# Early blocks as plain float32 matmuls, and modulation products moved out of the second mixer

## The chip, the core and the metric

The kernel runs on one core of a Trainium2 chip. The metric is the device time of one execution in microseconds (us); lower is better. TensorE multiplies matrices, VectorE (DVE), ScalarE (ACT) and GpSimd (POOL) do the work around it, and SyncE (SP) issues the DMAs that bring the weights from memory.

## What is computed

A trunk of two layers for 256 tokens and a model width of 2048, all in float32. In each layer a vector `c` gives six modulation vectors, and two sublayers, a mixer and a feed-forward with a short convolution, are each fed with a normed and modulated x:

```python
for i in range(DEPTH):
    mod = (c_act @ ada_w[i] + ada_b[i])[:, None, :]
    sh1, sc1, g1, sh2, sc2, g2 = jnp.split(mod, 6, axis=-1)
    h = rms_norm(x, norm_g[i, 0]) * (1.0 + sc1) + sh1
    y = even_mixer(h, ...) if i % 2 == 0 else odd_mixer(h, ...)
    x = x + g1 * y
    h = rms_norm(x, norm_g[i, 1]) * (1.0 + sc2) + sh2
    x = x + g2 * conv_ffn(h, ...)
```

The first mixer is a convolution beside a sparse attention; the second is a sliding-window attention (projections q, k, v) beside a gated unit (projections u and v). The feed-forward is `(silu(a) * b) @ w_down`, where a and b are 44 blocks of 128 columns each of `h @ w_up`, passed through a convolution over three tokens.

## The kernel before

Activations stand transposed: x is 16 tiles of 128 channels by 256 tokens, `xT[:, kt]`. A product with a weight block of 128 columns takes 16 steps over kt and adds up in one PSUM bank of 128x256; there are eight banks.

**Split weights.** From the first feed-forward on, float32 accuracy comes from three matmuls of the type float32r: a weight piece `raw` of up to 1024 columns is copied to `whi` (ScalarE, line 133), the rest `raw - whi` goes to `wlo` (line 139, VectorE or, for a quarter of the columns, GpSimd), the activation is split likewise, and `mm_t` issues hi x hi, hi x lo and lo x hi (lines 346 to 348). A piece that is wanted with `split=False` is multiplied as it is, by one plain float32 matmul (line 350); the first mixer works so. `take()` hands out the next piece, splits two pieces ahead and loads further ahead; three buffers each hold `raw`, `whi` and `wlo`. A raw buffer of a split piece is free when the split is done, one of a plain piece when TensorE has read it.

**Early blocks.** A sublayer could begin only when all of x is known and normed. `Modulated.outer` (FIRST = 7 blocks) runs ahead of that: it multiplies x, scaled by its gain but not yet normed, with seven blocks of weights at once, kt on the outside, into seven banks; two further columns carry the shift. `raw(kt)` makes the scaled x in a tile `hr` (lines 475 to 478), one kt ahead. At kt 3 the tokens' sums of squares go through TensorE, at kt 5 the reciprocal roots are spread over the partitions (`on_all`, line 409, from the `diag` tiles of line 408), and from then on the normed `h` of the later blocks is made beside it in `begin` and `end` (`hn` line 520, `hf` line 523, `h` lines 526 and 531). Early blocks stand at the head of the first feed-forward, the second mixer (its u projection) and the second feed-forward.

**Modulation products.** Each of the 192 columns of the modulation is one DVE instruction over 128x2048 (line 269, `ada`), with a DMA of 1 MB into one of two buffers ahead of it. No planner places them: each `take()` adds `rate["ada"]`, a number per stage, to a credit, and a full credit emits one product. A product that is needed and not there is emitted on the spot (`modulation`). In `outer` the rate is zero.

The order on every engine is that of the program text; engines wait for each other by semaphores only. The feed-forward works in four quarters: `h` blocks (two passes over 16 kt per gated block), then 16 output tiles `g` from the quarter's gated blocks, each added into x with its gate (line 545).

Of the kernel before, what the change touches and what calls it, by code (L numbers as in the profile page):

```python
# [8 lines left out]
F32 = mybir.dt.float32  # L9
F32R = mybir.dt.float32r  # L10
I32 = mybir.dt.int32
AF = mybir.ActivationFunctionType
ALU = mybir.AluOpType
# [3 lines left out]
P = 128  # L17
D = 2048
T = 256
NT = 2  # L20
KD = D // P
# [2 lines left out]
NQ = 4  # L24
QK = KF // NQ
FIRST = 7
HEADS = 8
NC = 15
L = 32
# [21 lines left out]
STATS = 3  # L51
SPREAD = 2
ADA_O = 0.0
LO_O = 0.25
LO_A = 0.25
ADA_A = 0.25
CONV_A = 0
# [13 lines left out]
ADA_1 = 0.5  # L71
ADA_2 = 0.5
ADA_3 = 0.6
ADA_F0S = 0.4
ADA_F0U = 0.4
ADA_F0D = 0.2
ADA_L1 = 0.5
ADA_F1 = 0.2
CONV = 1.6
ADA_OUT = 0.45  # L80
LO_L1 = 0.25
# [71 lines left out]
def trunk(ctx, tc, a, out):  # L153
# [11 lines left out]
    def bank():  # L165
        return psum.tile([P, 512], F32, tag="bank", name="bank")
# [26 lines left out]

    def want_ffn(i):
        for k in range(KD // 2):
            W.want(a["wup1"][i, k], 2, FIRST * P)
        for b in range(2 * QK - FIRST):
            W.want(a["wup2"][i, b], KD, P)
        for q in range(NQ):
            for j in range(q * QK, (q + 1) * QK):  # L200
                if q:
                    for ab in range(2):
                        W.want(a["wup"][i, j - QK, ab], KD, P)
            for kt in range(KD):
                W.want(a["wdn"][i, q, kt], QK, P)
# [21 lines left out]
    want_out(0)  # L227
    want_ffn(0)
    for k in range(KD // 2):
        W.want(a["od_u1"][k], 2, FIRST * P)  # L230
    W.want(a["od_kv"], KD, 512)
    for c in range(2):
        W.want(a["od_q"][c], KD, 512)
    for c in range(2):
        W.want(a["od_v"][c], KD, 512)
    for c in range(8 - FIRST):
        W.want(a["od_u2"][c], KD, P)
    want_out(1)
    want_ffn(1)
# [207 lines left out]
    class Modulated:  # L447
# [18 lines left out]
        def raw(self, kt):  # L466

            while self.nraw <= min(kt + 1, KD - 1):
                n = self.nraw
                self.nraw += 1  # L470
                gs, sh = self.gain(n)
                x = xT[:, n]
                h = hm.tile([P, 4 * T], F32R, tag="hm", name="hr")[:, :2 * T + 4].rearrange("p (a b) -> p a b", a=2)
                h = h[:, :, :T + 2]
                S.activation(h[:, 0, :T], x, AF.Copy, scale=gs)
                S.activation(h[:, 0, T:], sh.to_broadcast([P, 2]), AF.Copy)  # L476
                V.scalar_tensor_tensor(h[:, 1, :T], x, gs, h[:, 0, :T].bitcast(F32), op0=ALU.mult, op1=ALU.subtract)
                V.tensor_sub(h[:, 1, T:], sh.to_broadcast([P, 2]), h[:, 0, T:].bitcast(F32))
                self.raws.append(h)
            return self.raws[kt]  # L480

        def outer(self, n):

            first = [bank()[:, :T + 2] for _ in range(n)]
            r = None
            ada_rate, rate["ada"] = rate["ada"], ADA_O
            share, W.share = W.share, LO_O
            for kt in range(KD):
                x = self.raw(kt)
                w, _ = take()  # L490
                if kt == STATS:
                    drain()
                    r = token_rstd()
                if kt == STATS + SPREAD:
                    self.bc = on_all(r)
                for b in range(n):
                    s_ = slice(b * P, (b + 1) * P)
                    mm_t(first[b], w, s_, x, kt == 0, kt == KD - 1)
                k0 = STATS + SPREAD
                if kt >= k0:  # L500
                    for k in range(KD * (kt - k0) // (KD - k0), KD * (kt + 1 - k0) // (KD - k0)):
                        self(k)
            rate["ada"], W.share = ada_rate, share
            return first

        def begin(self):
            kt = self.n
            self.n += 1
            gs, sh = self.gain(kt)
            t = sm.tile([P, T], F32, tag="hn", name="hn")  # L510
            if self.whole:
                if kt % 4 == 0:
                    self.tiles.append(hm.tile([P, 4, T], F32, tag="hm", name="hw"))
                V.tensor_tensor(t, xT[:, kt], self.bc, op=ALU.mult)
                S.activation(self.tiles[-1][:, kt % 4], t, AF.Identity, bias=sh, scale=gs)
                return
            if kt % 2 == 0:
                self.tiles.append(hm.tile([P, 2, 2, T], F32R, tag="hm", name="h"))
            h = self.tiles[-1][:, kt % 2]
            V.tensor_tensor(t, xT[:, kt], self.bc, op=ALU.mult)  # L520
            f = sm.tile([P, T], F32, tag="hf", name="hf")
            if self.raws:
                V.tensor_scalar(f, t, gs, sh, op0=ALU.mult, op1=ALU.add)
            else:
                S.activation(f, t, AF.Identity, bias=sh, scale=gs)
            S.activation(h[:, 0], t, AF.Identity, bias=sh, scale=gs)
            self.open.append((h, f))

# [745 lines left out]
    with tc.tile_pool(name="l1", bufs=2) as lp:  # L1274
# [49 lines left out]
            return [squares, scaled, roped, roped_rest, None, turned]  # L1324


        first = h.outer(FIRST)
        us = [lp.tile([P, T], F32, tag="gu", name="gu", bufs=8) for _ in range(8)]
        colu = lp.tile([P, FIRST], F32, name="colu", bufs=1)
        for c in range(FIRST):  # L1330
            def norm_u(c=c):
                V.tensor_copy(colu[:, c:c + 1], first[c][:, T:T + 1])
                V.tensor_tensor(us[c], first[c][:, :T], h.bc, op=ALU.mult)

            waiting.append([norm_u])
# [116 lines left out]
        def centred():  # L1452
            e = sm.tile([P, NT], F32, tag="bve", name="bve")
            V.tensor_scalar(e, mv[:, :, 1], EPS, None, op0=ALU.add)
            r = rsqrt(e, NT)
            for t in range(NT):
                V.tensor_scalar(v[:, t], v[:, t], mv[:, t, 0:1], r[:, t:t + 1], op0=ALU.subtract, op1=ALU.mult)
# [7 lines left out]
        def gelu_u(c0, c1):  # L1465
            for c in range(c0, c1):
                S.activation(us[c], us[c], AF.Gelu_apprx_tanh, bias=colu[:, c:c + 1])

        hooks.extend([lambda: (drain(), gelu(0)), lambda: (gelu(1), stats(0)), lambda: (stats(1), gelu_u(0, 3)),
                      lambda: (centred(), gelu_u(3, FIRST))])  # L1470
        for j in range(2):
            for t in range(NT):
                hooks.append(lambda j=j, t=t: affine(j, t))
# [6 lines left out]
                            op=ALU.add)  # L1480
            V.tensor_tensor(us[c], y.rearrange("p t k -> p (t k)"), us[c], op=ALU.mult)

        for c in range(FIRST, 8):
            o = proj_t(h)
            defer(lambda o=o, c=c: S.activation(us[c], o, AF.Gelu_apprx_tanh))
        for c in range(8):
# [11 lines left out]
def layout(inputs):  # L1498
# [15 lines left out]
    def outer(w):  # L1514

        n, k = w.shape[-4], w.shape[-2]
        w = np.moveaxis(w, (-2, -3, -4), (-4, -3, -2))
        w = w.reshape(w.shape[:-4] + (k // 2, 2, P, n * P))
        return c(np.moveaxis(w, -3, -2)).reshape(w.shape[:-4] + (k // 2, P, 2 * n * P))
# [6 lines left out]
    a = {}  # L1526
# [33 lines left out]
    a["od_q"] = np.stack([rows(w[:, :512]), rows(w[:, 512:1024])])  # L1560
    a["od_kv"] = rows(w[:, 1024:1536])
    u = blocks(w[:, 1536:2560])
    a["od_u1"] = outer(u.reshape(8, P, KD, P)[:FIRST])
    a["od_u2"] = u[FIRST:]
    a["od_v"] = np.stack([rows(w[:, 2560:3072]), rows(w[:, 3072:])])
    a["sinks"] = x["od_sinks"]
    a["od_ln"] = np.concatenate([x["od_gmlp_ln_g"], x["od_gmlp_ln_b"]], axis=1)
# [28 lines left out]
```

## Time and profile before

| | |
|---|---|
| median of 3 runs | 2472.28 us (2468.01 to 2473.61) |
| the profiled execution | 2473.23 us |
| its span, first to last instruction | 2471.5 us |
| early blocks, first feed-forward | 512 to 582 us |
| rest of the first feed-forward | 582 to 1329 us |
| early blocks, second mixer | 1329 to 1391 us |
| rest of the second mixer | 1391 to 1675 us |
| early blocks, second feed-forward | 1675 to 1739 us |
| rest of the second feed-forward | 1739 to 2468 us |

The page sums busy time by engine, shows the span in 40 slices, follows the chain of work that ended last, and lists groups of instructions by line. TensorE is the engine to follow: it is busy in nearly all slices, and a stretch in which it isn't, or in which its granted clock is under 1, is where time can be had or lost. The windows view gives the same for any stretch, and the timeline shows instructions one by one, with the idle time before one and the engine that ended it.

### The profile page before, as it was taken

The page shows a single profiled execution, that of the slowest core. Times are in us where ns is not written, and L with a number is a line of the kernel's source. Part 1 is how long each engine was busy: PE and PEld are TensorE (multiplying, and loading weights), DVE is VectorE, ACT ScalarE, POOL GpSimd, SP SyncE. Part 2 cuts the span into 40 slices and gives each one's busy share as a digit, 9 for nine tenths or more (in the row PEclk, how much of TensorE's full clock was granted, in tenths as well). Part 3 has the DMA queues.
Part 4 walks back from the last instruction along what each step waited for, and adds up shares of the span by engine and source line. Part 5 has one row for each costly group of instructions (what it writes and reads, how often), then busy time and mean ns, then how long its engine had stood idle before and what let it go on. Part 6 is the DMA issues. An engine that isn't in the chain of part 4 may idle for free.

```text
span 2471.5 us, 40821 instructions
## 1 busy us (share of the span) xinstructions
PE 2313.7 (94%) x16372; PEld 2148.3 (87%) x16372; DVE 1761.4 (71%) x2768; ACT 1053.3 (43%) x1801; POOL 609.3 (25%) x340
## 2 busy tenths in 40 slices
PE   6899998987999999999999888887999999999999
PEld 3476777887999999999998767887999999999999
DVE  7757799669978878877887689687854554554554
ACT  2021353144534534544444445444644444444443
POOL 4233525011222222222222232121122112212121
PEclk9999999998999999999999989899999999999999
DMA  9968654855878878878876475563445545545545
GB/s 384 426 224 349 250 202 184 324 196 219 323 259 339 323 275 331 318 275 326 331 271 241 139 275 225 174 230 126 169 158 202 184 157 206 180 164 203 178 162 173
DMA packets 96385, 597.71 MB, mean 242 GB/s; under 512 B 11329, under 2 KB 14017, under 8 KB 44225
## 3 DMA queue, kind: packets, MB, share of 16 engines
q1 hardware_dynamic: 96194, 595.10, 64.9%
q8 instruction: 128, 2.10, 0.3%
q14 instruction: 63, 0.52, 0.1%
HBM read 592.96 MB, written 2.10 MB: 241 GB/s over the span
## 4 chain that ended last, share of the span: by engine, by line
PE 70%; DVE 18%; DMA 5%; ACT 3%; issue 3%; POOL 1%; SPq 0%; ACTq 0%; POOLq 0%; DVEq 0%
PE bank L347 19%; PE bank L348 19%; PE bank L346 19%; PE bank L350 7%; DVE ada L269 4%; DVE wlo L139 3%; DMA raw<-ev 2%; ACT whi L133 2%; PE bank L361 1%; POOL wlo L139 1%; DVE cy L937 1%; DVE h L531 1%; DVE ye L937 1%; DMA normg<-normg 1%; PE bank L357 1%
## 5 line engine op out<-in xcount | busy, mean ns | idle before, releaser
L133 ACT ACTIVATE whi<-raw 128x1024 fp32r<-128x1024 f32 (+3 forms) x705 | 669.9, 950 | 864.5 <-PE bank L347 768.7
L139 DVE TENSOR_TENSOR wlo<-raw,whi 128x1024 fp32r<-128x1024 f32 (+2 forms) x530 | 602.4, 1137 | 416.5 <-ACT whi L133 416.3
L139 POOL TENSOR_TENSOR wlo<-raw,whi 128x1024 fp32r<-128x1024 f32 (+3 forms) x175 | 418.5, 2391 | 1586.0 <-ACT whi L133 1412.8
L348 PE MATMUL bank<-h,wlo 128*128 128x256 f32 x2608 | 740.9, 284 | 7.4 <-DVE wlo L139 5.9
L346 PE MATMUL bank<-h,whi 128*128 128x256 f32 x2608 | 740.0, 284 | 0.0
L347 PE MATMUL bank<-h,whi 128*128 128x256 f32 x2608 | 739.6, 284 | 0.0
L348 PEld LDWEIGHTS bank<-h,wlo 128*128 128x128 f32 x2608 | 502.3, 193 | 9.8 <-DVE wlo L139 7.1
L347 PEld LDWEIGHTS bank<-h,whi 128*128 128x128 f32 x2608 | 502.5, 193 | 0.0
L346 PEld LDWEIGHTS bank<-h,whi 128*128 128x128 f32 x2608 | 502.4, 193 | 0.0
L269 DVE CUSTOM_DVE_ANT_0 ada<-ada,cB,adab 128x2048 f32<-128x2048 f32 x192 | 461.8, 2409 | 22.7 <-DMA ada<-adaw 22.1
L346 PE MATMUL bank<-g,whi 128*128 128x256 f32 x1408 | 401.8, 285 | 6.8 <-ACT g L668 6.8
L347 PE MATMUL bank<-g,whi 128*128 128x256 f32 x1408 | 402.0, 286 | 4.8 <-DVE g L669 4.5
L348 PE MATMUL bank<-g,wlo 128*128 128x256 f32 x1408 | 402.5, 286 | 0.3
L346 PEld LDWEIGHTS bank<-g,whi 128*128 128x128 f32 x1408 | 273.0, 194 | 7.6 <-ACT g L668 7.6
L347 PEld LDWEIGHTS bank<-g,whi 128*128 128x128 f32 x1408 | 272.9, 194 | 6.4 <-DVE g L669 6.4
L348 PEld LDWEIGHTS bank<-g,wlo 128*128 128x128 f32 x1408 | 273.0, 194 | 2.5 <-POOL wlo L139 1.8
L350 PE MATMUL bank<-hw,raw 128*128 128x256 f32 x640 | 149.9, 388 | 13.8 <-DMA raw<-ev 9.0
L350 PEld LDWEIGHTS bank<-hw,raw 128*128 128x128 f32 x640 | 121.5, 194 | 42.7 <-issue 19.4
L657 DVE SCALAR_TENSOR_TENSOR y<-bank,fcw,y 128x255 f32<-128x255 f32 x162 | 77.5, 478 | 97.0 <-ACT y L656 96.9
L346 PE MATMUL bank<-hr,whi 128*128 128x258 f32 x336 | 104.2, 310 | 26.4 <-ACT hr L476 26.4
L350 PE MATMUL bank<-mixw,raw 128*128 128x256 f32 x512 | 115.0, 388 | 4.8 <-DMA raw<-out 4.8
L361 PE MATMUL bank<-raw,hw 128*128 128x512 f32 (+1 forms) x320 | 117.3, 520 | 1.3 <-DMA raw<-ev_v 1.3
(267 smaller groups left out, 2855.4 us busy)
## 6 DMA issues: line engine op xcount, KB each, us to landing
ada<-adaw SPq DMA_DIRECT2D x192, 1024.0 KB, 5.8
raw<-wup SPq DMA_DIRECT2D x162, 1024.0 KB, 5.0
raw<-wdn SPq DMA_DIRECT2D x128, 704.0 KB, 4.2
raw<-out SPq DMA_DIRECT2D x44, 512.0 KB, 4.3
raw<-ev_a SPq DMA_DIRECT2D x16, 1024.0 KB, 5.1
raw<-ev SPq DMA_DIRECT2D x16, 896.0 KB, 14.7
raw<-wup SPq DMA_DIRECT2D x16, 896.0 KB, 4.6
raw<-cmp_w SPq DMA_DIRECT2D x8, 1024.0 KB, 8.6
```

Source lines behind the costliest of these rows:

```text
L133: nc.scalar.activation(hi[:, :n], raw, AF.Copy)
L139: eng.tensor_sub(lo[:, :n], raw, hi[:, :n].bitcast(F32))
L269: V.tensor_tensor_reduce(w, w, cB, 1.0, adab[:, i * 96 + j:i * 96 + j + 1], ALU.mult, ALU.add, m)
L346: PE.matmul(o, hi[:, s_], x[:, 0], start=start, stop=False)
L347: PE.matmul(o, hi[:, s_], x[:, 1], start=False, stop=False)
L348: PE.matmul(o, lo[:, s_], x[:, 0], start=False, stop=stop)
L350: PE.matmul(o, w[:, s_], x, start=start, stop=stop)
L357: PE.matmul(o[t], x[:, 0, ts_], hi[:, s_], start=start, stop=False)
L361: PE.matmul(o[t], x[:, ts_], w[:, s_], start=start, stop=stop)
L531: V.tensor_sub(h[:, 1], f, h[:, 0].bitcast(F32))
L657: V.scalar_tensor_tensor(y[:, 1:], o[:, :T - 1], w[:, 1:2], y[:, 1:], op0=ALU.mult, op1=ALU.add)
L937: V.scalar_tensor_tensor(d, xp[:, j:j + T], w, d, op0=ALU.mult, op1=ALU.add)
```

## The change

The early blocks' weights and the scaled x are no longer split: `wup1` and `od_u1` are wanted with `split=False`, `hr` is a plain float32 tile of 257 columns made by two ScalarE instructions, and one plain matmul of 257 columns stands for three of 258. `hf` is made on ScalarE instead of VectorE. The second mixer has six early blocks instead of seven; its seventh and eighth u block come later, split. The modulation rates are set anew: higher in the first feed-forward, zero in the second mixer, lower in the second feed-forward.

```diff
+FIRST_U = 6
...
-LO_O = 0.25
...
-ADA_F0S = 0.4
-ADA_F0U = 0.4
-ADA_F0D = 0.2
-ADA_L1 = 0.5
-ADA_F1 = 0.2
+ADA_F0S = 0.45
+ADA_F0U = 0.42
+ADA_F0D = 0.22
+ADA_L1 = 0.0
+ADA_F1 = 0.1
...
-            W.want(a["wup1"][i, k], 2, FIRST * P)
+            W.want(a["wup1"][i, k], 2, FIRST * P, split=False)
...
-        W.want(a["od_u1"][k], 2, FIRST * P)
+        W.want(a["od_u1"][k], 2, FIRST_U * P, split=False)
...
-    for c in range(8 - FIRST):
+    for c in range(8 - FIRST_U):
...
-                h = hm.tile([P, 4 * T], F32R, tag="hm", name="hr")[:, :2 * T + 4].rearrange("p (a b) -> p a b", a=2)
-                h = h[:, :, :T + 2]
-                S.activation(h[:, 0, :T], x, AF.Copy, scale=gs)
-                S.activation(h[:, 0, T:], sh.to_broadcast([P, 2]), AF.Copy)
-                V.scalar_tensor_tensor(h[:, 1, :T], x, gs, h[:, 0, :T].bitcast(F32), op0=ALU.mult, op1=ALU.subtract)
-                V.tensor_sub(h[:, 1, T:], sh.to_broadcast([P, 2]), h[:, 0, T:].bitcast(F32))
+                h = hm.tile([P, 4 * T], F32, tag="hm", name="hr")[:, :T + 1]
+                S.activation(h[:, :T], x, AF.Copy, scale=gs)
+                S.activation(h[:, T:], sh, AF.Copy)
...
-            first = [bank()[:, :T + 2] for _ in range(n)]
+            first = [bank()[:, :T + 1] for _ in range(n)]
...
-            share, W.share = W.share, LO_O
...
-            if self.raws:
-                V.tensor_scalar(f, t, gs, sh, op0=ALU.mult, op1=ALU.add)
-            else:
-                S.activation(f, t, AF.Identity, bias=sh, scale=gs)
+            S.activation(f, t, AF.Identity, bias=sh, scale=gs)
...
-        first = h.outer(FIRST)
+        first = h.outer(FIRST_U)
...
-        for c in range(FIRST, 8):
+        for c in range(FIRST_U, 8):
```

VectorE in the early blocks of the second feed-forward, one step and a half, before (896 columns are a piece of seven blocks):

```order
L520 TENSOR_TENSOR hn<-xT,bc 128x256
L523 TENSOR_SCALAR hf<-hn,gs,mod 128x256
L531 TENSOR_TENSOR h<-hf,h 128x256
L462 SCALAR_TENSOR_TENSOR gs<-mod,normg 128x1
L477 SCALAR_TENSOR_TENSOR hr<-xT,gs,hr 128x256
L478 TENSOR_TENSOR hr<-mod,hr 128x2
L139 TENSOR_TENSOR wlo<-raw,whi 128x896
L520 TENSOR_TENSOR hn<-xT,bc 128x256
L523 TENSOR_SCALAR hf<-hn,gs,mod 128x256
L531 TENSOR_TENSOR h<-hf,h 128x256
```

and after:

```order
L516 TENSOR_TENSOR hn<-xT,bc 128x256
L524 TENSOR_TENSOR h<-hf,h 128x256
L462 SCALAR_TENSOR_TENSOR gs<-mod,normg 128x1
L516 TENSOR_TENSOR hn<-xT,bc 128x256
L524 TENSOR_TENSOR h<-hf,h 128x256
```

The `hr`, `wlo` and `hf` rows are gone from VectorE; the `hn` and `h` rows stay.

VectorE in the second mixer, between the scaling of the first query projection (`n`), its rotation (`n` with `cc` and `nrw`) and the weight splits, before:

```order
L603 SCALAR_TENSOR_TENSOR n_13212<-bank,rsy,gains_12181 128x128 x8
L269 ISA ada,mod<-ada,cB,adab 128x2048
L269 ISA mod 128x1
L139 TENSOR_TENSOR wlo<-raw,whi 128x1024
L612 TENSOR_TENSOR n_13212<-n_13212,cc 128x512
L613 TENSOR_TENSOR n_13212<-n_13212,nrw 128x512
L612 TENSOR_TENSOR n_13212<-n_13212,cc 128x512
L613 TENSOR_TENSOR n_13212<-n_13212,nrw 128x512
L139 TENSOR_TENSOR wlo<-raw,whi 128x1024
L269 ISA ada,mod<-ada,cB,adab 128x2048
L269 ISA mod 128x1
L139 TENSOR_TENSOR wlo<-raw,whi 128x1024
```

and after:

```order
L596 SCALAR_TENSOR_TENSOR n_12562<-bank,rsy,gains_11868 128x128 x8
L139 TENSOR_TENSOR wlo<-raw,whi 128x1024
L605 TENSOR_TENSOR n_12562<-n_12562,cc 128x512
L606 TENSOR_TENSOR n_12562<-n_12562,nrw 128x512
L605 TENSOR_TENSOR n_12562<-n_12562,cc 128x512
L606 TENSOR_TENSOR n_12562<-n_12562,nrw 128x512
L139 TENSOR_TENSOR wlo<-raw,whi 128x1024 x4
```

Each `ada` row is a modulation product, and the `mod` row its result; all 23 that stood in the second mixer are gone from it. Of them and of the others, the first feed-forward has seven more, and the second, which had none, has sixteen.

VectorE in the first quarter of the second feed-forward, where output tiles are added into x, before:

```order
L139 TENSOR_TENSOR wlo<-raw,whi 128x640
L545 SCALAR_TENSOR_TENSOR xT<-bank,mod,xT 128x256
L139 TENSOR_TENSOR wlo<-raw,whi 128x768
L139 TENSOR_TENSOR wlo<-raw,whi 128x640
L545 SCALAR_TENSOR_TENSOR xT<-bank,mod,xT 128x256
```

and after:

```order
L538 SCALAR_TENSOR_TENSOR xT<-bank,mod,xT 128x256
L139 TENSOR_TENSOR wlo<-raw,whi 128x768
L269 ISA ada,mod<-ada,cB,adab 128x2048
L269 ISA mod 128x1
L139 TENSOR_TENSOR wlo<-raw,whi 128x640
L538 SCALAR_TENSOR_TENSOR xT<-bank,mod,xT 128x256
L139 TENSOR_TENSOR wlo<-raw,whi 128x768
L269 ISA ada,mod<-ada,cB,adab 128x2048
L269 ISA mod 128x1
```

Three of the sixteen products come before the first output tile, and thirteen stand in this quarter, nearly one for each further tile. In the first feed-forward a product now stands between `y<-y`, the last gating of a quarter, and the subtraction `g<-y,g` behind it, in the first and the third quarter; it stood ahead of that block before.

## Rows read from the trace of the kernel before

**Rows 1.** The page's first row and two of its groups: busy us, mean ns, idle before

```profile
span 2471.5 us, 40821 instructions
...
L269 DVE CUSTOM_DVE_ANT_0 ada<-ada,cB,adab 128x2048 f32<-128x2048 f32 x192 | 461.8, 2409 | 22.7 <-DMA ada<-adaw 22.1
...
L350 PE MATMUL bank<-mixw,raw 128*128 128x256 f32 x512 | 115.0, 388 | 4.8 <-DMA raw<-out 4.8
```

**Rows 2.** Windows by stage: length, busy time of each engine, granted clock, DMA share, GB/s

```profile
core 0: us, PE busy (x) PEld busy (x) DVE busy (x) ACT busy (x) POOL busy (x), PEclk, DMA share, GB/s
512.00:582.30 70.30, 52.15 (x347) 48.95 (x346) 55.70 (x123) 30.74 (x59) 8.94 (x4) 0.85 0.49 185
676.80:745.00 68.20, 66.35 (x531) 65.24 (x530) 49.67 (x57) 26.77 (x34) 21.17 (x8) 0.97 0.73 270
745.00:871.90 126.90, 126.90 (x1058) 126.72 (x1057) 107.51 (x132) 62.54 (x86) 30.03 (x12) 1.00 0.86 327
1329.40:1391.20 61.80, 48.58 (x347) 45.79 (x345) 48.32 (x116) 31.71 (x61) 9.71 (x5) 0.92 0.46 161
1391.20:1560.80 169.60, 147.04 (x638) 119.34 (x637) 138.82 (x268) 78.30 (x167) 42.16 (x29) 0.90 0.62 229
1560.80:1675.20 114.40, 102.60 (x803) 101.16 (x802) 81.62 (x124) 47.66 (x78) 23.93 (x9) 0.94 0.57 198
1675.20:1739.40 64.20, 48.84 (x347) 45.84 (x346) 50.03 (x122) 32.20 (x62) 8.76 (x4) 0.92 0.34 121
1828.70:1893.60 64.90, 63.76 (x531) 63.56 (x530) 30.61 (x43) 26.78 (x35) 14.54 (x8) 1.00 0.57 194
```

**Rows 3.** TensorE's timeline around the first early blocks: start, us, [idle before <- releaser]

```profile
494.66 17.43 PE L350 MATMUL bank<-mixw,raw 128*128 128x256 f32 x80
...
512.05 0.28 PE L347 MATMUL bank<-hr,whi 128*128 128x258 f32 x1
...
519.46 0.28 PE L348 MATMUL bank<-hr,wlo 128*128 128x258 f32 x1
...
529.73 0.68 PE L409 MATMUL bank<-diag,onesm 128*128 128x128 f32 x4 [4.45 <-DVE diag L408]
...
530.37 0.41 PE L347 MATMUL bank<-hr,whi 128*128 128x258 f32 x1
...
533.16 0.42 PE L348 MATMUL bank<-hr,wlo 128*128 128x258 f32 x1
```

**Rows 4.** VectorE's timeline, one step of the same early blocks

```profile
541.93 0.48 DVE L477 SCALAR_TENSOR_TENSOR hr<-xT,gs,hr 128x256 fp32r<-128x256 f32 x1 [0.58 <-ACT hr L475]
542.33 0.15 DVE L478 TENSOR_TENSOR hr<-mod,hr 128x2 fp32r<-128x2 f32 x1
542.86 1.09 DVE L139 TENSOR_TENSOR wlo<-raw,whi 128x896 fp32r<-128x896 f32 x1 [0.38 <-ACT whi L133]
...
544.33 0.41 DVE L523 TENSOR_SCALAR hf<-hn,gs,mod 128x256 f32<-128x256 f32 x1
544.66 0.42 DVE L531 TENSOR_TENSOR h<-hf,h 128x256 fp32r<-128x256 f32 x1
```

**Rows 5.** TensorE's waits, 1391 to 1675 us: waiter, releaser, us in total, times, longest

```profile
PE bank L620 <- DVE n L613: 9.4, 3, 6.2
PE bank L347 <- DVE mix L339: 5.9, 4, 2.3
PE bank L1394 <- ACT sc L1387: 5.2, 1, 5.2
PE bank L1477 <- DVE gv L1463: 4.8, 2, 3.1
PE bank L357 <- DVE gu L1333: 2.6, 1, 2.6
PE bank L1402 <- DVE su L1382: 2.5, 1, 2.5
```

**Rows 6.** Windows again: a stretch of low clock, and the busiest stretch of the DMA engines

```profile
530.40:533.80 3.40, 3.40 (x19) 3.40 (x18) 2.67 (x8) 1.80 (x4) 0.00 (x0) 0.50 0.71 257
40.00:110.00 70.00, 62.57 (x163) 30.07 (x162) 58.67 (x70) 7.21 (x12) 35.92 (x19) 1.00 1.01 427
```

More of the change, by code (lines that the diff above doesn't have):

```diff
@@ L502, in outer @@
                         self(k)
-            rate["ada"], W.share = ada_rate, share
+            rate["ada"] = ada_rate
             return first
@@ L1324, in heads @@
             return [squares, scaled, roped, roped_rest, None, turned]
-        first = h.outer(FIRST)
+        first = h.outer(FIRST_U)
         us = [lp.tile([P, T], F32, tag="gu", name="gu", bufs=8) for _ in range(8)]
-        colu = lp.tile([P, FIRST], F32, name="colu", bufs=1)
-        for c in range(FIRST):
+        colu = lp.tile([P, FIRST_U], F32, name="colu", bufs=1)
+        for c in range(FIRST_U):
             def norm_u(c=c):
@@ L1469, in trunk @@
         hooks.extend([lambda: (drain(), gelu(0)), lambda: (gelu(1), stats(0)), lambda: (stats(1), gelu_u(0, 3)),
-                      lambda: (centred(), gelu_u(3, FIRST))])
+                      lambda: (centred(), gelu_u(3, FIRST_U))])
         for j in range(2):
@@ L1562, in layout @@
     u = blocks(w[:, 1536:2560])
-    a["od_u1"] = outer(u.reshape(8, P, KD, P)[:FIRST])
-    a["od_u2"] = u[FIRST:]
+    a["od_u1"] = outer(u.reshape(8, P, KD, P)[:FIRST_U])
+    a["od_u2"] = u[FIRST_U:]
     a["od_v"] = np.stack([rows(w[:, 2560:3072]), rows(w[:, 3072:])])
```

## The prediction

> **What bounds the kernel now.** I read the windows by stage first, then the timeline at the places where TensorE is idle, then its waits. The program up to 512 us is the same before and after, so only what follows counts. In the full stages of a feed-forward TensorE is the bound: 126.90 us busy of 126.90 [rows 2]. There is little to gain there, and anything that holds TensorE up costs its full length. Five stretches are different [rows 2]: the three with early blocks (70.3, 61.8 and 64.2 us, TensorE busy for 52.15, 48.58 and 48.84, granted clock 0.85 to 0.92), and the rest of the second mixer (169.6 and 114.4 us at clocks of 0.90 and 0.94). There TensorE waits for VectorE, and after a wait the clock falls: behind the wait of 4.45 us at 529.73 [rows 3] stands a window at 0.50 [rows 6]. In it the float32r matmuls go at (533.16 - 530.37) / 13 = 0.215 us apart, at full clock at (519.46 - 512.05) / 61 = 0.1215 us [rows 3]. So a wait costs its length, and then some more of the low clock.
>
> **The price of a plain matmul.** The plain float32 matmul stands in the trace of before: 80 records of the output projection start at 494.66 and take 17.43 us [rows 3]. A matmul leaves two records: 512 of them [rows 1] for the 256 that the code issues there. Without the last record's tail of some 0.39 us [rows 1] that is 17.04 / 79 = 0.216 us a record and 0.432 us a matmul of 256 columns, so 0.433 of 257. The three float32r matmuls that it replaces take 3 x 0.1215 = 0.365. On TensorE alone the change therefore loses 112 x 0.068 = 8 us in a feed-forward's early blocks; it can win only by taking waits away. The Trainium skill ("FP8 and Floating Point Precision", TensorE Precision Notes) says that true float32 takes four passes through the array. By the step of one float32r pass that would be 0.486 us, 17 us more over the 320 plain matmuls, and speaks against the change; the two records at 0.216 us are what this trace shows.
>
> **The early blocks, part by part.** A step of VectorE was: the low half of the scaled x (0.48 and 0.15 us, after 0.58 of waiting for ScalarE), the low half of a weight piece (1.09 us, after a wait of 0.38), `hf` (0.41), `h` (0.42), and `hn` and the gain that stay [rows 4]. All but `hn`, `h` and the gain go. `hf` now costs ScalarE as much as `h`, and the scaled x no longer hands over to VectorE; ScalarE was busy for 30.74 of 70.3 us [rows 2], and loses its copies of the weights. What remains on VectorE in a step is under 1.5 us, against 7 x 0.433 = 3.03 us of TensorE, so TensorE becomes the bound. The root of the sums of squares has two steps, 6 us, between its two TensorE visits; its chain of small instructions took longer than two of the old, shorter steps only because the splits stood in between. A raw buffer is now held until TensorE has read it, but the load behind it then has two loads' worth of TensorE, 12 us, to land.
> In the first feed-forward: 112 x 0.433 = 48.5 us and some 1.2 for the sums and the spread roots (0.68 for the second [rows 3], less for the first), 49.7 against 70.3 [rows 2]: -20.6. Four modulation products are still made on the spot in its last steps, and the last two can only load once the first two are used; I add 1.5 us for that (0 to 5). Second feed-forward: 49.7 against 64.2, -14.5. Second mixer, six blocks: 96 x 0.433 + 1.2 = 42.8 against 61.8, -19.0. The u block that comes later takes 48 float32r matmuls at 126.90 / 1058 = 0.12 us [rows 2], +5.8. Together, with the 1.5, -46.8.
>
> **The second mixer without products.** 23 products at 2.41 us [rows 1] leave VectorE, 55 us of its 138.82 + 81.62 [rows 2]. What TensorE gets of that I take wait by wait [rows 5]. The 5.9 us for the split of `mix` go: two products stood among four of these short splits. The 2.6 us for `gu` go too, since six early blocks leave two banks free for the next projection instead of one. Of the 9.4 us for the rotated n, the waits for the keys go and the longest, 6.2, shrinks by the product ahead of it: 5.7 off. Of `sc` (5.2) 1.2 goes, since ScalarE's copy ahead of it ends no earlier; of `su` (2.5) 2.4. The 4.8 us for `gv` stay: a load and two long additions set them. That is 17.8 us. Low clock cost 10% of 169.6 and 6% of 114.4, 24 us, beside the 30.4 us of these waits and some smaller ones, so 0.7 us for each; so 17.8 x 1.7 = 30 us. The ends: 8.5 (only `mix` and `gu`, with no clock back) and 50 (all but `gv` and its clock).
>
> **Where the products go.** The first feed-forward gets seven. In its `h` quarters VectorE is busy for 107.51 of 126.9 [rows 2] and takes one more each; free, hidden under TensorE. The first `h` blocks, where VectorE still works off the early ones: +1 (0 to 4). At the end of the first and third quarter a product of 2.41 us now stands between the last gating and the split that TensorE needs: at most 2.4 each with some clock, at least nothing; I take +2 each, +4.
> The second feed-forward gets 16: three beside its first `h` blocks, +2 (0 to 5), and 13 in its first down quarter. There an output tile has 64.9 / 16 = 4.06 us; VectorE's own work is 30.61 / 16 = 1.91 [rows 2], with a product 4.32, so 0.26 us over, 3.5 in all, less one tile of lead. The loads: 1.05 MB for a product and 0.72 for weights each 4.06 us is 436 GB/s, and the highest that the trace shows over a long stretch is 427 [rows 6]: 0.08 us over per tile, 1 in all. VectorE is in order: a product that waits for its load holds up the weight splits behind it, and TensorE behind those. I take +4 (0 to 31, each product in full).
>
> **The sum.** -46.8 - 30 + 1 + 4 + 2 + 4 = -65.8 us. The profiled execution took 2473.23 us, 1.7 over its span of 2471.5 [rows 1] and 1 over the median. That gives 2407.
>
> **The rivals.** *The mixer keeps its waits*: chains of ScalarE, GpSimd and VectorE set them, not the products. For it: `n` waits also for two GpSimd instructions, `sc` for ScalarE. Only 8.5 us are won: 2407 + 21.5 = 2429.
> *The down quarter is the new wait*: loads land late at 436 GB/s, and half of the 13 x 2.41 us is felt, 15.7 instead of 4, with the two quarter ends at twice their price: 2407 + 11.7 + 4 = 2423. For it is the DMA sum above; against it, two products and two loads are there ahead.
> *Four passes*: a plain matmul takes four steps of a float32r one, 4 x 0.1215 = 0.486 us, if a moving x of 257 columns streams less well than one of 256: 2407 + 17 = 2424. Against it: 80 records in a row at 0.216. It is the case in which the rule quoted from the Trainium skill would set the time; the trace agrees with it only in that a plain matmul costs more than three float32r ones (0.432 against 0.365).
> *Low clock in the plain blocks, slower*: if these stages ran at the clock of 0.50, a matmul would take 2 x 0.433 = 0.866 us, the way that float32r went from 0.1215 to 0.215. Three stages would take 277 + 3.6 = 281 us instead of 196.3, +85 in place of -52.6: 2407 + 137 = 2544. It turns slower only from a mean of some 0.64 us a matmul on: 2473 - 2407 = 66 over 320 is 0.206 above 0.433. Against it: the low clock follows waits here, and the 80 records in a row ran at full pace.
>
> **How the numbers follow.** Forecast 0.62, mixer 0.16, down quarter 0.12, four passes 0.06, low clock 0.04. The forecast's own range, from the ends of its terms taken partly together, is 2390 to 2423; the next three cases lie at 2423, 2424 and 2429, so the range is 2390 to 2432. A measurement can tell 0.2%, 5 us, from no change. All cases but the last are faster by more; some of the last, and of mishaps that add up, is within or above: faster 0.94, same 0.02, slower 0.04.
>
> **What would show it.** Right: early stretches of some 50, 43 and 50 us with TensorE busy throughout, clock near 1 and plain records 0.217 us apart; no VectorE `wlo` in them; in the mixer no wait for `mix` and hardly any for `gu`; in the first down quarter of the second feed-forward VectorE over 90% busy and a length of 65 to 70 us instead of 64.9; quarter ends one and three of the first feed-forward with a wait of some 3 us for `g`. Wrong: TensorE waiting for `hr` or for raw weights inside the early blocks, plain records further apart, the mixer's waits as long as before, or a down quarter over 75 us.

## The result, and the profile after

The changed kernel takes 2410.0 us (median of 4 runs, 2408.22 to 2416.22), the kernel before 2470.15 us beside it (4 runs, the three of the section above among them): a ratio of 0.976, 95% interval 0.9737 to 0.9782. The forecast was 2407, the range 2390 to 2432. The profiled execution has a span of 2408.7 us against 2471.5 [rows 1], 62.8 less.

From the page after: the span, the modulation product, and the plain matmul of the early blocks, which wasn't there before (busy us, mean ns, idle before):

```profile
span 2408.7 us, 39982 instructions
...
L269 DVE CUSTOM_DVE_ANT_0 ada<-ada,cB,adab 128x2048 f32<-128x2048 f32 x192 | 462.5, 2412 | 28.9 <-DMA ada<-adaw 28.2
...
L350 PE MATMUL bank<-hr,raw 128*128 128x257 f32 x640 | 140.4, 380 | 0.0
```

The 640 records stand for 320 plain matmuls, and TensorE was idle ahead of them for 0.0 us in all three feeds together. The windows by stage of the kernel after (columns as in [rows 2]); in order: first early blocks, first `h` blocks behind them, the second mixer's early blocks, its two remaining parts, the last early blocks, the second feed-forward's first `h` blocks, its first down quarter:

```profile
515.10:564.50 49.40, 49.40 (x234) 43.43 (x233) 26.47 (x70) 24.61 (x61) 2.37 (x1) 1.00 0.61 219
564.50:662.90 98.40, 90.98 (x722) 90.27 (x721) 93.57 (x125) 51.73 (x81) 24.34 (x7) 0.95 0.77 295
1315.40:1357.90 42.50, 42.50 (x203) 37.38 (x202) 17.95 (x63) 24.90 (x62) 2.36 (x1) 1.00 0.55 190
1357.90:1513.00 155.10, 144.27 (x687) 120.19 (x686) 102.90 (x237) 82.70 (x178) 39.16 (x29) 0.96 0.42 149
1513.00:1617.60 104.60, 99.42 (x801) 97.93 (x800) 60.58 (x103) 43.22 (x70) 18.42 (x8) 0.97 0.53 176
1617.60:1667.00 49.40, 49.40 (x234) 43.42 (x234) 19.55 (x66) 26.86 (x65) 2.05 (x1) 1.00 0.38 136
1667.00:1755.30 88.30, 86.97 (x722) 86.56 (x721) 70.34 (x106) 50.52 (x79) 18.55 (x8) 1.00 0.57 206
1755.30:1829.90 74.60, 68.57 (x530) 66.86 (x529) 61.15 (x67) 26.00 (x34) 17.96 (x8) 0.95 0.86 322
```

Against [rows 2]: the early stretches fell from 70.3, 61.8 and 64.2 us to 49.4, 42.5 and 49.4, with TensorE busy throughout at the full granted clock. The mixer's rest fell from 169.6 + 114.4 to 155.1 + 104.6, although one u block of 5.8 us moved into it. The last window grew: 64.9 us before, 74.6 now, at a granted clock of 0.95 where it was 1.00.

Below, the length of a stage is the time from its first matmul to the last, read from each kernel's trace (some tenths above the windows).

| stage, us | before | after | changed by |
|---|---|---|---|
| early blocks, three stretches | 70.6, 61.9, 64.3 | 49.6, 42.7, 49.6 | -54.9 |
| first feed-forward, first `h` blocks | 94.8 | 98.7 | +3.9 |
| its four down quarters | 272.4 | 273.0 | +0.6 |
| second mixer, the rest (with the u block) | 284.3 | 260.2 | -24.1 |
| second feed-forward, first `h` blocks | 89.5 | 88.6 | -0.9 |
| its first down quarter | 65.0 | 74.7 | +9.7 |
| the next `h` blocks | 126.9 | 127.9 | +1.0 |
| start of the first early blocks | 511.7 | 515.1 | +3.4 |

The last line isn't the change's: kernels that are the same up to there began their early blocks anywhere from 509.5 to 516.5 us in the runs below. That is the scatter of one execution, and why single spans are read here stage by stage.

### The profile page after: what moved, and what is told of

Read it like the earlier page. It is cut to its first block, busy times and chain, and to the rows that moved or that the text cites. A ratio compares the mean times of both kernels' runs of the same rounds, so it can differ in the third digit from the quotient of the medians.

```text
span 2408.7 us, 39982 instructions
## 1 busy us (share of the span) xinstructions
PE 2303.3 (96%) x16052; PEld 2134.6 (89%) x16052; DVE 1663.0 (69%) x2587; ACT 1029.5 (43%) x1803; POOL 575.0 (24%) x329
## 5 line engine op out<-in xcount | busy, mean ns | idle before, releaser
L133 ACT ACTIVATE whi<-raw 128x1024 fp32r<-128x1024 f32 (+2 forms) x659 | 626.4, 952 | 859.1 <-PE bank L347 727.9
L139 DVE TENSOR_TENSOR wlo<-raw,whi 128x1024 fp32r<-128x1024 f32 (+2 forms) x495 | 560.1, 1133 | 410.5 <-ACT whi L133 410.2
L139 POOL TENSOR_TENSOR wlo<-raw,whi 128x1024 fp32r<-128x1024 f32 (+2 forms) x164 | 389.4, 2374 | 1558.8 <-ACT whi L133 1504.5
L350 PE MATMUL bank<-hr,raw 128*128 128x257 f32 x640 | 140.4, 380 | 0.0
L350 PEld LDWEIGHTS bank<-hr,raw 128*128 128x128 f32 x640 | 121.0, 190 | 16.6
```

What stands on the lines that cost most here:

```text
L133: nc.scalar.activation(hi[:, :n], raw, AF.Copy)
L139: eng.tensor_sub(lo[:, :n], raw, hi[:, :n].bitcast(F32))
L350: PE.matmul(o, w[:, s_], x, start=start, stop=stop)
```

## The experiments

Three parts can be had one by one: plain early blocks, new rates for the modulation products, six early blocks in the mixer instead of seven. The changed kernel with seven blocks is

```diff
-FIRST_U = 6
+FIRST_U = 7
```

and with the rates of the kernel before it is

```diff
-ADA_F0S = 0.45
-ADA_F0U = 0.42
-ADA_F0D = 0.22
-ADA_L1 = 0.0
-ADA_F1 = 0.1
+ADA_F0S = 0.4
+ADA_F0U = 0.4
+ADA_F0D = 0.2
+ADA_L1 = 0.5
+ADA_F1 = 0.2
```

Both edits together give the first kernel below (plain early blocks, seven of them, old rates). The second is the kernel before with the new rates alone, the third the changed kernel with seven blocks, and the fourth the changed kernel with the old rates. What counts as plain early blocks, the weights, the scaled x and `hf` on ScalarE, stayed one part and was not taken apart further.

**Early blocks alone.**

> The changed kernel with its plain early blocks, but seven of them in the second mixer and the modulation rates of before: the first part of the change alone. Theory (the three early stretches and the products' places each give their own part, and the parts add up): the early stretches take 49.6 us each, against 70.6, 61.9 and 64.3 before, so 48 us less than before, some 2422; the rest of the second mixer as long as before (284 us), the first down quarter of the second feed-forward at 65. Rival (the products in the mixer cost nothing by themselves; its waits came from the late end of the early blocks): the rest of the mixer shrinks here too, by 20 us or more, and the time is near 2400.

2417.5 us, ratio 0.9788 (0.9767 to 0.9809), nearer to the theory's 2422 than to 2400. All three stretches are 49.6 us long, 48 us less than before in the three together. The rest of the mixer takes 276.4 us, 8 less than the 284 that the theory expected but far from the rival's 20, and the whole kernel 52 us less. TensorE's waits in that rest:

```profile
PE bank L613 <- DVE n L606: 9.8, 4, 6.2
PE bank L347 <- DVE mix L339: 6.0, 4, 2.3
PE bank L1387 <- ACT sc L1380: 5.2, 1, 5.2
PE bank L1395 <- DVE pT L1389: 5.2, 5, 2.5
PE bank L1470 <- DVE gv L1456: 4.3, 2, 2.7
PE bank L348 <- POOL wlo L139: 1.1, 1, 1.1
```

The waits for `n`, `mix` and `sc` are as long as before [rows 5]; the one for `gu` is gone.

**New rates alone.**

> The kernel before with the changed modulation rates only; early blocks split and seven. Theory: early stretches as before (70, 62, 64 us), the rest of the second mixer 24 us shorter (its waits for the split of mix, for the rotated n and for su go), the first feed-forward 4 us longer, the first down quarter of the second one 9 us longer: some 2459, 11 us less than before. Rival (the products were hidden in the mixer): the mixer less than 8 us shorter, the time 2470 or above.

2470.3 us, ratio 1.0 (0.9989 to 1.0011): nothing, where the theory expected 2459. The traces show a gain that is given back. The mixer's rest fell from 284.3 to 261.9 us, while the second feed-forward's first `h` blocks grew by 2.1, its first down quarter by 8.2 (65.0 to 73.2) and the `h` blocks behind by 3.8, and its early blocks by 1.0. By stages that leaves -22.4 + 15.1 = -7.3 in this execution, of which its later start of the early blocks took 3.5. The other 4 us are not a gain either: the profiled execution of the kernel before took 3.7 us more than the median of the 13 runs of that kernel beside this one, and the medians differ by 0.8. Two of the mixer's waits in this kernel:

```profile
PE bank L357 <- DVE gu L1333: 2.6, 1, 2.6
PE bank L347 <- DVE mix L339: 2.6, 2, 1.8
```

The wait for `gu` stands here as before, 2.6 us [rows 5], without a product in the mixer. In the early-only kernel, with products and seven blocks, there is none at all. So this wait goes with the split form of the early blocks, not with the number of free banks.

**Seven blocks with the new rates, twice.**

> The changed kernel with seven early blocks in the second mixer instead of six. Theory (two free banks instead of one take away the wait behind the early blocks): the early stretch 49.6 instead of 42.7 us, 5.8 us less for the later block, and a wait of 2 to 3 us for gu with low clock behind it is back: 3 to 7 us slower than the changed kernel, 2413 to 2417. Rival (the number of blocks doesn't matter, as a block costs TensorE 6.9 us early and 5.8 late): no such wait, within 1.5 us of the changed kernel.

> The changed kernel with seven early blocks in the second mixer, beside the changed kernel with its six. By the stages of the earlier profiles six blocks are worth only 1.7 us in the mixer (6.9 us of plain matmuls against 5.8 of float32r ones, and 0.6 elsewhere); the 8 us by which the two medians differed were scatter of the feed-forward before. So 2412 beside 2410. The rival: six blocks spare a wait that later stages feel as well, and the 8 us come back: 2418 beside 2410.

> The changed kernel again, beside the next three on one chip. Expected 2410 (2408 to 2414), as the comparison showed it. Its start of the first early blocks, 509 to 516 us in the runs so far, is expected to vary without any change in the program.

2418.4 us and 2415.1 for seven blocks, 2410.0 and 2412.7 for the changed kernel: 8.4 apart the first time, 2.4 the second, with overlapping intervals (0.9763 to 0.9791, and 0.9743 to 0.9779, in the second). No wait for `gu` came back with seven blocks, so the theory of the first of these expectations has its mechanism wrong. By stages early blocks and mixer take 1.7 us less with six in the one pair (302.9 against 304.6) and 6.3 in the other (300.4 against 306.7). So six blocks are worth some 2 to 8 us by the medians with the new rates; that is not clear of the scatter.

**Six blocks with the old rates.**

> Plain early blocks and six of them in the second mixer, with the old rates (products in the second mixer, none in the first down quarter of the second feed-forward). If the new rates are worth nothing, since what the mixer gains the down quarter and the clock around it give back, this lands with the changed kernel within 3 us, 2410 to 2413, and lower than with seven blocks by 2 to 8. If the new rates do their part only with six blocks, it stays at 2416 to 2418, like the version with seven blocks and old rates (2417.5).

2423.7 us, ratio 0.9808 (0.9794 to 0.9822): worse than either reading, and 6 above seven blocks with these rates. This is where the rates do their work, 11 to 14 us between 2423.7 and 2410.0 or 2412.7. TensorE's waits in the mixer's rest of this kernel (waiter, releaser, us in total, times, longest):

```profile
PE bank L347 <- DVE mix L339: 11.8, 4, 5.2
PE bank L613 <- DVE n L606: 9.8, 4, 6.2
PE bank L1470 <- DVE gv L1456: 5.7, 2, 4.2
PE bank L1387 <- ACT sc L1380: 5.0, 1, 5.0
PE bank L1395 <- DVE pT L1389: 5.0, 5, 2.5
```

and of the kernel after, which differs in the rates alone:

```profile
PE bank L613 <- DVE n L606: 5.1, 4, 3.9
PE bank L1470 <- DVE gv L1456: 4.1, 2, 2.7
PE bank L1387 <- ACT sc L1380: 4.0, 1, 4.0
PE bank L1395 <- DVE pT L1389: 1.7, 3, 0.7
PE bank L347 <- DVE mix L339: 1.0, 2, 0.5
```

37.3 us of waits against 15.9, and the rest of the mixer takes 168.5 + 121.3 us against 155.3 + 104.9, 29.6 less. The `mix` line is the clearest. VectorE's and GpSimd's timelines of the old-rates kernel, where TensorE's longest `mix` wait is (start, us, and idle before):

```profile
1599.64 2.35 DVE L269 CUSTOM_DVE_ANT_0 ada<-ada,cB,adab 128x2048 f32<-128x2048 f32 x1
...
1601.91 2.56 DVE L339 TENSOR_TENSOR mix<-gu,mix 128x256 fp32r<-128x256 f32 x1
```

```profile
1600.34 3.84 POOL L139 TENSOR_TENSOR wlo<-raw,whi 128x1024 fp32r<-128x1024 f32 x1 [11.42 <-ACT whi L133]
```

The product stands ahead of the split that TensorE waits for, and the split, 0.42 us elsewhere, takes 2.56 because GpSimd's split of a weight piece is still running (the last section has more such meetings). Why six blocks put the products in a worse place among the `mix` splits than seven (121.3 us against 114.1) was not followed further. With seven blocks the rates shorten the mixer's rest as well, from 276.4 to 255.0 us in these profiles, but the table shows that the time as a whole doesn't fall.

| us, median | old rates | new rates |
|---|---|---|
| splits in the early blocks (before) | 2470.2, 2469.5 | 2470.3 |
| plain, seven blocks | 2417.5 | 2418.4, 2415.1 |
| plain, six blocks | 2423.7 | 2410.0, 2412.7 |

**What the second feed-forward's first down quarter waits for.** There 12 products stand beside 16 output tiles (by the trace the thirteenth starts 2 us behind the quarter). Three kernels change only the last 16 products:

```diff
-            nc.sync.dma_start(w, a["adaw"][i, j])
+            if (i, j) < (1, 80):
+                nc.sync.dma_start(w, a["adaw"][i, j])
```

where the product then reads `cB` in place of what was loaded; the loads as before, but the product over `n` columns alone,

```diff
+        n = D if (i, j) < (1, 80) else 64
-        V.tensor_tensor_reduce(w, w, cB, 1.0, adab[:, i * 96 + j:i * 96 + j + 1], ALU.mult, ALU.add, m)
+        V.tensor_tensor_reduce(w[:, :n], w[:, :n], cB[:, :n], 1.0, adab[:, i * 96 + j:i * 96 + j + 1], ALU.mult, ALU.add, m)
```

and the next load not behind the product but at the step that takes the next weight piece:

```diff
-        ada_load(source[1])
+        if (i, j) < (1, 78):
+            ada_load(source[1])
+        else:
+            owed.append(1)
...
+        if owed:
+            owed.clear()
+            ada_load(source[1])
```

> The changed kernel where the sixteen products of the second feed-forward read no weights from memory (they multiply the vector by itself; the loads are left out, so their sixteen columns of the modulation are others). Theory (in the first down quarter the loads, and the weight loads queued behind them on SP, hold TensorE up): the quarter falls from 74.7 to 67 us or less. Rival (VectorE's 13 products of 2.4 us hold it up): it stays above 71.

> The changed kernel where the sixteen products of the second feed-forward take all their loads, but multiply only 64 of 2048 columns (so their sixteen columns of the modulation are others). Theory (loads and the SP queue): VectorE is relieved, but the loads still cost: the quarter stays above 70 us; if the queue is held up by the product's own length, since the next load waits for its end, it falls part of the way. Rival (VectorE's time): it falls to 66 or less.

> The changed kernel where the load for a later product of the second feed-forward's sixteen is issued one weight piece later, behind that piece's own weight load on SP, not right behind the product. Theory (a weight load queued on SP behind a load that waits for the product's end comes late): the first down quarter falls from 74.7 to 70 us or less. Rival (the queue's order doesn't matter, only VectorE's time or the bytes): within 2 us of 74.7.

One run each: 2404.6, 2399.6 and 2415.7 us. The quarter's windows without the loads, and with the loads but 64 columns:

```profile
1754.00:1824.80 70.80, 66.53 (x531) 65.22 (x529) 63.30 (x67) 26.84 (x35) 20.75 (x8) 0.98 0.51 176
```

```profile
1749.60:1815.80 66.20, 64.76 (x529) 63.60 (x528) 32.52 (x66) 24.77 (x33) 11.82 (x7) 1.00 0.87 339
```

Of the 9.7 us lost, 5.9 remain without any load, with VectorE busy for 63.30 of 70.8 (89%). With all the loads but products of 64 columns only 1.1 remain, at the highest rate of the three, 339 GB/s. So VectorE's time is most of it: 5.9 alone, where the loads alone cost 1.1, and both together 9.7, so that the loads make it dearer by 3.8. Issuing the loads one piece later changed nothing for the better (75.9 us): this order of the two loads on SP is no cure, as the rival said.

VectorE's time itself is more than was added up. Its groups in this quarter by shape, before:

```profile
L139 DVE TENSOR_TENSOR wlo<-raw,whi 128x768 fp32r<-128x768 f32 x11 | 10.5, 958 | 11.5 <-ACT whi L133 11.5
L139 DVE TENSOR_TENSOR wlo<-raw,whi 128x640 fp32r<-128x640 f32 x12 | 9.9, 825 | 18.7 <-ACT whi L133 18.7
```

and after:

```profile
L269 DVE CUSTOM_DVE_ANT_0 ada<-ada,cB,adab 128x2048 f32<-128x2048 f32 x12 | 28.1, 2345 | 3.6 <-DMA ada<-adaw 3.6
L139 DVE TENSOR_TENSOR wlo<-raw,whi 128x768 fp32r<-128x768 f32 x12 | 14.3, 1190 | 3.4 <-ACT whi L133 3.3
L139 DVE TENSOR_TENSOR wlo<-raw,whi 128x640 fp32r<-128x640 f32 x11 | 11.7, 1063 | 3.3 <-ACT whi L133 3.3
```

The products cost 28.1 us as planned. But the same splits went from 958 and 825 ns to 1190 and 1063: 12 x 0.232 + 11 x 0.238 = 5.4 us that no term had. Without the loads they are about as long (1131 and 1207 ns), so this is part of the 5.9. The last section shows where they come from.

**VectorE in the early blocks.** One split-sized instruction more in each of their 16 steps:

```diff
+                extra = wp.tile([P, PIECE], F32R, tag="wlo", name="extra", bufs=NSPLIT)
+                V.tensor_sub(extra[:, :n * P], w[:, :n * P], cB[:, :n * P])
```

> The changed kernel with one more VectorE instruction in every step of the early blocks: a subtraction of 128x896 (768 in the mixer) from the plain weights into a scratch tile that nobody reads, as long as the low half of a weight piece was. Theory A (what held TensorE up was the chain of hand-overs through VectorE and ScalarE, not VectorE's busy time): the early stretches stay at 49.6, 42.7 and 49.6 us, within 2 us, though VectorE is busy for 37 to 45 us of 50. Theory B (VectorE's busy time was the bound): they grow by 5 us or more each.

2416.7 us in one run. The second and third stretch stay at 42.7 and 49.6 us, so the 12 to 14 us that VectorE was busy longer there (30.23 against 17.95 and 33.53 against 19.55 in the windows) are free. That is less than the 37 to 45 us that were meant to be tried, and than the 48 and 50 before the change [rows 2]: what a VectorE as full as then would do beside plain blocks isn't shown. The first grows from 49.6 to 58.1: one wait of TensorE takes 6.1 of it, behind which the mean granted clock of the stretch is 0.94. VectorE's timeline shows what stood at its source, two products that had to be loaded on the spot:

```profile
PE bank L350 <- ACT hr L475: 6.1, 1, 6.1
```

```profile
557.78 2.35 DVE L269 CUSTOM_DVE_ANT_0 ada<-ada,cB,adab 128x2048 f32<-128x2048 f32 x1 [1.02 <-DMA ada<-adaw]
...
562.91 2.35 DVE L269 CUSTOM_DVE_ANT_0 ada<-ada,cB,adab 128x2048 f32<-128x2048 f32 x1 [2.77 <-DMA ada<-adaw]
```

In the changed kernel VectorE waits 0.25 and 0.23 us for the same two loads, and TensorE not at all: the lead that hides them there is only just long enough.

**Products into the early blocks.** If VectorE is free there, that is the place for the products which hurt the down quarter.

```diff
-ADA_O = 0.0
+ADA_O = 0.5
-ADA_F0S = 0.45
-ADA_F0U = 0.42
+ADA_F0S = 0.3
+ADA_F0U = 0.4
```

> The changed kernel with modulation products spread over the early blocks too (a rate of 0.5 there instead of 0, six to eight in each stretch), and fewer in the first feed-forward (0.3 and 0.4 instead of 0.45 and 0.42): all 192 are made before the first down quarter of the second feed-forward. Theory (VectorE has room in the early blocks now, 20 to 26 us busy of 50; where the products cost time is in the down quarter and behind the first early blocks): early stretches stay at 49.6, 42.7 and 49.6 us, the down quarter falls from 74.7 to 65, the first hidden blocks from 98.7 to 95 or less: some 2396. Rival (a product of 2.4 us in an early step delays the gains and the scaled x that TensorE waits for): the early stretches grow by 5 us or more each, and the time is 2408 or above.

2403.3 us, ratio 0.9724 (0.9698 to 0.975), between the two expectations. The early stretches stay at 49.6, 42.7 and 49.6 us and the down quarter is back at 64.9. But the first feed-forward's first `h` blocks fell only from 98.7 to 98.1, where 95 or less was expected, and the second's took 94.7 us instead of 88.6, with TensorE waiting for `wlo` up to 2.0 us right behind the early blocks. So the last kernel keeps products out of the last three early steps and out of the first six blocks behind them:

```diff
-ADA_O = 0.0
+ADA_O = 0.6
-ADA_F1 = 0.1
+ADA_F1 = 0.3
+QUIET = 6
...
+                if kt == KD - 3:
+                    rate["ada"] = 0.0
...
+            rate["ada"] = 0.0
             for b in range(FIRST, 2 * QK):
+                if b == FIRST + QUIET:
+                    rate["ada"] = split
```

> The changed kernel with products in the early blocks (0.6 of one a piece, none in the last three steps), none beside the first six projected blocks behind them, then 0.45 a block in the first feed-forward and 0.3 in the second; none is left for the first down quarter of the second feed-forward. If the waits for the low halves at the start of the first h quarters come from products among VectorE's splits there, these quarters lose 3 to 5 us each against the version with products in the early blocks at 0.5 throughout (2403.3), and the kernel takes 2393 to 2398. If VectorE is late there because of the early blocks' own norms, convolutions and gatings, it stays at 2401 to 2405.

2397.5 us (2396.4 to 2399.0), ratio 0.9702 (0.9688 to 0.9716): below both kernels and in the range of the first reading, though the two `h` stretches gained more than its 3 to 5 us, some 8 and 6. Whether the last early steps or the first six blocks did more, both kept free at once, isn't shown. The kernel's windows for the first feed-forward's first `h` blocks, the mixer's early blocks and the down quarter:

```profile
564.10:653.60 89.50, 87.61 (x722) 86.59 (x721) 82.21 (x120) 51.40 (x82) 19.13 (x8) 1.00 0.70 260
...
1304.90:1354.20 49.30, 45.58 (x202) 39.43 (x201) 35.26 (x78) 24.73 (x61) 2.36 (x1) 0.93 0.89 325
...
1753.20:1818.00 64.80, 63.93 (x531) 63.53 (x530) 29.75 (x43) 26.85 (x35) 14.23 (x8) 1.00 0.56 194
```

The first `h` blocks take 89.5 us against 98.4 after, and 5 less than before the change; TensorE's waits for VectorE's `wlo` in them are 1.4 us in all, against this in the kernel after:

```profile
PE bank L348 <- DVE wlo L139: 7.4, 3, 3.9
```

The price is a wait that wasn't there, in the mixer's early blocks: 42.7 became 49.5 (and the last early blocks 51 from 49.6), with this wait of TensorE at a mean clock of 0.93, and VectorE's timeline shows two products ahead of the `diag` at 1321.78, one that waits for its load and one right before it:

```profile
PE bank L410 <- DVE diag L409: 3.7, 1, 3.7
```

```profile
1314.85 2.35 DVE L270 CUSTOM_DVE_ANT_0 ada<-ada,cB,adab 128x2048 f32<-128x2048 f32 x1 [3.29 <-DMA ada<-adaw]
...
1319.51 2.35 DVE L270 CUSTOM_DVE_ANT_0 ada<-ada,cB,adab 128x2048 f32<-128x2048 f32 x1
...
1321.78 0.48 DVE L409 TENSOR_SCALAR diag<-ident,rsy 128x128 f32<-128x128 f32 x2
```

Keeping products out of that chain as well was not tried.

## The prediction, point by point

**Right: the price of a plain matmul.** Inside the early blocks 13 records take 2.98 us, so (2.98 - 0.38) / 12 = 0.217 us a record, with the 0.38 of the group's mean for the last one's length; that is 0.433 a matmul, as forecast. Four steps of 0.1215 would be 0.486, and the three stretches would be 17 us longer than they are.

```profile
534.58 2.98 PE L350 MATMUL bank<-hr,raw 128*128 128x257 f32 x13
```

**Right: the early blocks.** 49.7, 42.8 and 49.7 us were forecast, 49.6, 42.7 and 49.6 measured. The 1.5 for the four products made on the spot was not felt (the extra-work experiment shows how near it was). VectorE's `wlo` is gone from their steps, and the granted clock is 1.00 in all three.

**Right in size, wrong in one of its reasons: the second mixer, -30.** From before to after its rest changed by -29.9 us without the u block, and between the two kernels that differ in the rates alone by -29.6. The waits moved as worked out for `sc` (5.2 to 4.0) and `gv` (4.8 to 4.1); `mix` kept 1.0 of 5.9 and `n` 5.1 of 9.4 (3.7 expected). `gu` went, but not because two banks are free: it goes with seven blocks too, once the early blocks are plain. In all the six named waits, 30.4 us, became 14.2, 16.2 less where 17.8 were expected, and the clock, 0.90 and 0.94 before, 0.96 and 0.97 after, gave back more than the 0.7 us for each that was allowed. The rates alone, on the kernel before, bring 22.4 of the 30 and the plain early blocks alone 7.9: the term belongs to the two parts together, where the prediction gave it to the products.

**Mis-sized: the down quarter, +9.7 where +4 was taken.** The step that failed is VectorE's sum of 4.32 us a tile. It took the splits at their old length, and they became 29% longer at 640 columns and 24% at 768; and it expected VectorE over 90% busy, where it was 82% (61.15 of 74.6), since it also waited for products' loads (3.6 us) and for ScalarE's high halves. It also had no price for what stands behind a wait: TensorE's idle time grew by 4.9 us (from 64.90 - 63.76 to 74.60 - 68.57), its busy time for the same matmuls by 4.8, at a granted clock of 0.95 instead of 1.00. How much of that the clock alone costs isn't shown; the second profile of this kernel has 68.29 busy at 0.98. In it the quarter takes 75.2 us, just over the 75 that the prediction named as a sign of being wrong. The bound of 31 held, and the rival for this quarter (15.7) was too dark. The runs, one for each, price the parts: 5.9 VectorE, 3.8 the loads on top.

**Mis-sized: the first `h` blocks of the first feed-forward, +3.9 where +1 was taken.** The added product is not the cause: with the old rates these blocks take 99.1 and 98.1 us too. With a quiet start they take 89.9, and TensorE's waits for `wlo` fall from 7.4 to 1.4, so products among the weight splits there are what costs. Their place does, not their number: with 9 products these blocks take 89.9, with 10 in the kernel with products in the early blocks 98.1. That they cost more than before the change because shorter early blocks leave VectorE with more of its tail is a reading that no run tests.

**About right: quarter ends.** Waits for `g` of 1.8 and 3.3 us at the ends one and three were there as expected. Against the same kernel with old rates the four quarters cost 273.0 - 269.4 = 3.6 us more, +4 forecast; against the kernel before only 0.6. The second feed-forward's first `h` blocks came out at -0.9, not +2.

**The sum, close in part by luck.** -65.8 forecast, -62.8 in the spans. The two mis-sized terms cost 5.7 + 2.9 = 8.6 us more than allowed. The early blocks (2.3 better), the quarter ends (3.4, against before) and the second feed-forward's first `h` blocks (2.9) gave 8.6 back, and the late start of this execution took 3.4. That the total came so close is the luck of these small terms; the two large ones stand on their own.

## What to carry to other kernels

A step whose operand splits starve the matrix engine can be faster with the plain, dearer matmul: here 0.433 us against 0.365, and yet 48 us less in three stretches of seven blocks. Vector work that can be done at any time belongs where the matrix engine has its longest steps, and neither among short splits that it waits for, nor right behind a stretch from which VectorE still has a tail. A rate that gains 22 us in one stage can give them all back in another, so each is to be timed with the others in place.

## What the runs showed of the hardware that was not expected

In these traces a weight split on VectorE that starts while GpSimd runs one of its own is held up until GpSimd is done. In the down quarter of the kernel after, GpSimd and VectorE (start, us):

```profile
1791.62 1.98 POOL L139 TENSOR_TENSOR wlo<-raw,whi 128x768 fp32r<-128x768 f32 x1 [2.95 <-ACT whi L133]
```

```profile
1791.84 2.45 DVE L139 TENSOR_TENSOR wlo<-raw,whi 128x640 fp32r<-128x640 f32 x1
...
1797.16 0.83 DVE L139 TENSOR_TENSOR wlo<-raw,whi 128x640 fp32r<-128x640 f32 x1 [0.21 <-ACT whi L133]
```

GpSimd ends at 1793.60. VectorE's split of the same shape takes 0.83 us alone, and here ends at 1794.29, 0.69 after GpSimd. Five of VectorE's 23 splits of 640 and 768 columns in this quarter start inside a GpSimd split; together they take 5.5 us more than their shapes did before, and the other 18 no more than before. So these meetings are the 5.4 us that the forecast's sum lacked. An instruction with an input in PSUM was not held up: the add into x at 1787.35 takes its 0.48 us inside GpSimd's split of 1785.69 to 1788.67. The wait goes the other way too. Where a product has begun first, GpSimd's split takes longer:

```profile
1769.43 3.43 POOL L139 TENSOR_TENSOR wlo<-raw,whi 128x640 fp32r<-128x640 f32 x1 [6.29 <-ACT whi L133]
```

```profile
1769.08 2.34 DVE L269 CUSTOM_DVE_ANT_0 ada<-ada,cB,adab 128x2048 f32<-128x2048 f32 x1
```

The same shape took GpSimd 1.57 us in this quarter of the kernel before. Before the change VectorE was idle for 18.7 and 11.5 us ahead of such splits in this quarter, and they were not stretched; with a product in 12 of 16 tiles the two engines' splits meet. In the kernel with short products those of 640 columns are back at 825 ns. The Trainium skill ("SBUF — State Buffer", Who interferes with whom) says that a VectorE instruction with two inputs in SBUF contends with a GpSimd instruction that reads SBUF, that the ports they share are an exclusive lock, and that the order of issue decides who blocks. This trace agrees: VectorE's split ends 0.69 us after GpSimd's, GpSimd's (1772.86) some 1.4 us after the product (1771.42), about their own lengths.
